# Four 64x64 gate products in place of two 128x128 ones in a linear recurrence, with one gate's heads swapped in PSUM

## The chip, the cores and the metric

The kernel runs on one core of a Trainium2 chip. The metric is the device time of one execution in microseconds (us); the median of the runs is compared. An execution taken by the profiler has a time of its own and, inside it, the span of the trace from its first instruction to its last.

## The reference

One layer of a decoder trunk: an RMS norm, one input projection, four groups of heads beside each other (two kinds of attention, a delta-rule recurrence "RWKV-7", and a gated linear recurrence "RG-LRU"), each multiplied with a gate of its own, and one output projection with a residual and a last norm. x is 1 x 1024 x 1024, in float32. The change is in the linear recurrence, whose 256 channels are four heads of 64:

```python
xc = causal_depthwise_conv(x, conv_w) + conv_b
xh = xc.reshape(b, s, N_HEADS, HEAD_DIM)
r = sigmoid(einsum('bsni,nij->bsnj', xh, w_a).reshape(b, s, c) + b_a)   # first gate
i = sigmoid(einsum('bsni,nij->bsnj', xh, w_x).reshape(b, s, c) + b_x)   # second gate
log_a = -8 * r * softplus(-lam)
a = exp(log_a)
u = sqrt(-expm1(2 * log_a)) * (i * xc)
h_t = a_t * h_(t-1) + u_t
```

Each head has a 64x64 matrix of its own for each of the two gates.

## The kernel before, in words

Everything of one core is one program, in which each engine has its instructions in an order that is written out by hand: the table ORDERS holds for TensorE (PE), VectorE (DVE), ScalarE (ACT), GpSimd (POOL) and SyncE (SP) the places of their instructions, and each one is held behind the one ahead of it. So an engine can't pass a waiting instruction; it waits there.

TensorE's order is mixed. The projections (pj_..., L402 and L989) are long rows of full 128x128 products that depend on little, and they stand between the short products of the RWKV recurrence, which depend on each other: for each chunk of 64 positions px (L758), then X (ScalarE copies px out of PSUM, L767), pu and py, then UV (VectorE copies pu, L783), ph, then UV of the next chunk (VectorE adds, L796), and so on. The linear recurrence runs in the same stretch of time, about 225 to 300 us from the start. Its function lru is called four times: for each pair of heads pr (128 channels, on 128 partitions) and each half hf of 512 positions.

Of one call, in the order of its data: the convolution makes xc (ACT L1048, then three DVE instructions, L1050); lwg holds the pair's two 64x64 matrices of a gate on the diagonal of a 128x128 matrix whose other quarters are zero, so that one float32 product (L1056) makes a gate's input for both heads; ScalarE takes each through a sigmoid out of PSUM (L1057) into rt, whose first half is r and whose second is i. Then tanh (L1065, into xb), exp (L1066), square (L1067), sqrt (L1069) on ScalarE, L1063, L1068 and L1070 on VectorE, the scan (L1073) and the product with the output gate (L1075), and y_out splits the result in two parts (L850, L851) and stores it. The PSUM banks of the gates, lg, come from a pool of two buffers (gbk) which other products use as well.

A float32 product takes two passes through the array, which the trace shows as two MATMUL records each; products of the rounded type (fp32r) take one.

Of the kernel before, what the change touches and what calls it, by code (L numbers as in the profile page):

```python
# [16 lines left out]
P = 128  # L17
# [25 lines left out]
for _name, _w in (  # L43
# [23 lines left out]
        "852-857 2018 2019 858-870 2026 871-895 2027-2057 896-914 2058-2089 915-919 2020 2021 920-932 2090-2093 "  # L67
        "933-941 2094-2101 942-947 2102-2109 948-953 2110-2121 954-956 2022 2023 2122-2125 957-967 2130-2133 "
        "2126-2129 968-983 2134-2141 984-992 2142-2149 993-996 2150-2153 997-1004 2154-2161 1005-1011 2162-2169 "
        "1012-1015 2170-2173 1016 1017 2024 2025 2174-2181 1018-1029 2182-2189 1030-1032 2190-2193 1033-1037 "  # L70
        "2194-2201 1038-1043 2202-2209 1044-1051 2210-2213 1052-1055 2214-2221 1056-1065 2222-2229 1066-1068 "
        "2230-2233 1069-1073 2234-2241 1074-1087 2242-2245 1088-1143 2246-2261 1144-1245 2262-2264 1246-1250 "
        "2265-2267 1251-1271 2275-2280 1272-1285 2288-2290 2268-2270 2291-2293 1286 2271-2274 2309-2311 2281-2283 "
        "1287 2312-2314 1288-1291 2284-2287 1292-1294 2330 2331 1295-1297 2294-2297 1298 1299 2332-2334 1300 1301 "
        "2302-2304 1302-1304 2335 2336 1305 1306 2298-2301 1307 1308 2337-2339 1309-1311 2305-2308 1312 1313 2363 "
        "2364 1314 1315 2315-2318 1316-1318 2365-2367 1319 1320 2323-2325 1321 1322 2368 2369 1323-1325 2319-2322 "
        "1326 1327 2370-2372 1328 1329 2326-2329 1330-1332 2340-2343 1333 1334 2396 2397 1335 1336 2348-2351 "
        "1337-1339 2398-2400 1340 1341 2356-2358 1342 1343 2401 2402 1344-1346 2344-2347 1347 1348 2403-2405 1349 "
        "1350 2352-2355 1351-1353 2359-2362 1354 1355 2373-2376 1356 1357 2437 2438 1358-1360 2381-2384 1361 1362 "
        "2439-2441 1363 1364 2389-2391 1365-1367 2442 2443 1368 1369 2377-2380 1370 1371 2444-2446 1372-1374 "  # L80
        "2385-2388 1375 1376 2392-2395 1377 1378 2406-2409 1379 1380 2414-2417 1381-1383 2478-2480 1384-1388 "
        "2422-2425 2410-2413 1389 2430-2432 1390 1391 2481-2483 1392 1393 2418-2421 1394-1396 2426-2429 1397 1398 "
        "2433-2436 1399 1400 2447-2450 1401 1402 2455-2458 1403 1404 2491-2493 1405-1407 2463-2466 1408 1409 "
        "2451-2454 1410 1411 2471-2473 1412 1413 2494-2496 1414 1415 2459-2462 1416 1417 2467-2470 1418-1420 "
        "2474-2477 1421 1422 2504-2506 1423-1425 2484-2486 1426-1429 2507-2509 1430-1432 2487-2490 1433-1436 "
        "2525-2527 1437-1440 2497-2499 1441-1443 2528-2530 1444-1447 2500-2503 1448-1450 2546 2547 1451-1453 "
        "2510-2513 1454 1455 2548-2550 1456 1457 2518-2520 1458-1460 2551 2552 1461 1462 2514-2517 1463 1464 "
        "2553-2555 1465-1467 2521-2524 1468 1469 2579 2580 1470 1471 2531-2534 1472-1474 2581-2583 1475 1476 "
        "2539-2541 1477 1478 2584 2585 1479-1481 2535-2538 1482-1485 2586-2588 1486-1490 2542-2545 1491-1494 "
        "2556-2559 1495-1499 2612 2613 1500-1504 2564-2567 1505-1508 2614-2616 1509-1513 2572-2574 1514-1518 2617 "  # L90
        "2618 1519-1522 2560-2563 1523-1527 2619-2621 1528-1532 2568-2571 1533-1536 2575-2578 1537-1541 2589-2592 "
        "1542-1546 2653 2654 1547-1550 2597-2600 1551-1555 2655-2657 1556-1559 2605-2607 1560-1564 2658 2659 "
        "1565-1569 2593-2596 1570-1573 2660-2662 1574-1578 2601-2604 1579-1583 2608-2611 1584-1587 2622-2625 "
        "1588-1592 2630-2633 1593-1596 2982 2983 1597-1620 2638-2641 2626-2629 1621 1622 2646-2648 2984 2985 "
        "2634-2637 2642-2645 1623-1626 2649-2652 1627-1630 2663-2666 1631-1634 2671-2674 1635-1639 2993 2994 "
        "1640-1644 2679-2682 1645-1647 2667-2670 1648-1652 2687-2689 1653-1656 2995 2996 1657-1660 2675-2678 "
        "1661-1664 2683-2686 1665-1669 2690-2693 1670-1673 3004 3005 2694-2696 2986-2988 2697-2700 3006 3007 "
        "2701-2703 2989-2992 2704-2706 3023 3024 2707-2709 2997-2999 2710-2713 3025 3026 2714-2716 3000-3003 "
        "2717-2719 3042 3043 2720 2721 3008-3011 2722-2724 3044 3045 2725 2726 3016-3018 2727 2728 3046 3047 2729 "
        "2730 3012-3015 2731 2732 3048 3049 2733 2734 3019-3022 2735-2737 3073 3074 2738 2739 3027-3030 2740 2741 "  # L100
        "3075 3076 2742 2743 3035-3037 2744 2745 3077 3078 2746-2748 3031-3034 2749 2750 3079 3080 2751 2752 "
        "3038-3041 2753 2754 3050-3053 2755 2756 3104 3105 2757 2758 3058-3061 2759-2761 3106 3107 2762 2763 "
        "3066-3068 2764 2765 3108 3109 2766 2767 3054-3057 2768 2769 3110 3111 2770 2771 3062-3065 2772-2774 "
        "3069-3072 2775 2776 3081-3084 2777 2778 3143 3144 2779 2780 3089-3092 2781 2782 3145 3146 2783 2784 "
        "3097-3099 2785-2787 3147 3148 2788 2789 3085-3088 2790 2791 3149 3150 2792 2793 3093-3096 2794 2795 "
        "3100-3103 2796 2797 3112-3115 2798-2800 3182 3183 2801 2802 3120-3123 2803 2804 3184 3185 2805-2807 "
        "3128-3131 2808 3116-3119 2809 2810 3186 3187 2811 2812 3136-3138 2813 2814 3124-3127 2815 2816 3188 3189 "
        "2817 2818 3132-3135 2819 2820 3139-3142 2821 2822 3151-3154 2823 2824 3221 3222 2825 2826 3159-3162 2827 "
        "2828 3223 3224 2829-2836 3167-3170 3155-3158 3225 3226 3175-3177 2837-2839 3163-3166 2840 2841 3227 3228 "
        "2842 2843 3171-3174 2844 2845 3178-3181 2846 2847 3190-3193 2848 2849 3284 3285 2850 2851 3198-3201 2852 "  # L110
        "3286 3287 2853 2854 3206-3209 2855 2856 3194-3197 2857 2858 3288 3289 2859 2860 3214-3216 2861 2862 "
        "3202-3205 2863 2864 3290 3291 2865 2866 3210-3213 2867 2868 3217-3220 2869 2870 3229-3232 2871 2872 3315 "
        "3316 2873 2874 3237-3240 2875 2876 3317 3318 2877 2878 3245-3248 2879 2880 3233-3236 2881 3319 3320 2882 "
        "2883 3253-3255 2884 2885 3241-3244 2886 2887 3321 3322 2888 2889 3249-3252 2890 2891 3256-3259 2892 2893 "
        "3292-3295 2894 2895 3370 3371 2896-2898 3300-3303 2899 2900 3308-3310 2901 2902 3296-3299 2903-2905 3372 "
        "3373 2906 2907 3304-3307 2908-2910 3311-3314 2911 2912 3323-3326 2913 2914 3389 3390 2915-2917 3331-3334 "
        "2918 2919 3339-3341 2920 2921 3327-3330 2922-2924 3391 3392 2925 2926 3335-3338 2927 2928 3342-3345 "
        "2929-2931 3374-3377 2932 2933 3432 3433 2934-2936 3382-3384 2937 2938 3434 3435 2939 2940 3378-3381 "
        "2941-2943 3385-3388 2944 2945 3393-3396 2946-2948 3443 3444 2949 2950 3401-3403 2951-2953 3445 3446 2954 "
        "2955 3397-3400 2956 2957 3404-3407 2958-2960 3436-3438 2961-2965 3439-3442 2966-2970 3447-3449 2971-2976 "  # L120
        "3450-3453 2977-2981 3260-3283 3346-3369 3408-3431 3454-3477"
# [38 lines left out]
        "1 0 2 4 7 8 3 9 5 10 6 11-21 23 24 27 31-35 22 36 25 28 26 37 29 38 30 49 39 40 63 41 43 64 42 44 80 48 "  # L160
        "81 45 46 82 50 51 47 52 53 83 84 59-61 54 62 55-57 85 75 86 65 58 66 87 67 69 68 70 88 74 71 72 89 90 "
        "178 91 73 92 179 93 76-79 94 190 180 181 95 182 184 183 185 189 96 97 186-188 98 99 191-193 195 194 272 "
        "196 273 197 198 200 100 101 199 102 235 103-107 110 111 202-204 108 274 275 205 114 206 207 115 208 109 "
        "209 210 219 211 220 112 221-224 201 212 225 118 119 213 226 236 227 229 113 239 228 231 232 230 122 233 "
        "234 214 116 237 240 215 241 242 117 216 217 123 245 238 120 218 124 248 243 125 246 121 247 276 249 254 "
        "244 250 277 126 251 257 127 252 278 255 128 256 258 259 279 263 129 260 266 253 281 280 264 261 130 265 "
# [1384 lines left out]
```

## Time and profile before

| What | Value |
|---|---|
| Median of 3 runs | 629.45 us (625.92 to 630.3) |
| Profiled execution | 629.03 us |
| Span of its trace | 627.1 us |
| Granted TensorE clock | 0.992 |
| PE busy | 608.5 us, 97% |
| DVE busy | 489.8 us, 78% |
| ACT busy | 390.7 us, 62% |
| POOL busy | 200.8 us, 32% |
| The gates' products (L1056) | 16 records of 591 to 664 ns, first at 238.3 us, last at 282.5 us |
| The gates' sigmoids (L1057) | 8 of 670 to 688 ns |

Times in a row are us from the span's start, durations us or ns as said there. A MATMUL record holds the whole way of a product through the array, so records overlap, and the distance from one start to the next says more than a duration. In brackets behind a row stands how long the engine sat idle before it, and what it waited for.

### The profile page before, as it was taken

To read this page: it belongs to the slowest core of one execution; us is meant where nothing else is said; L and a number is where in the kernel's file an instruction comes from. 1 tells how busy PE (TensorE), PEld (TensorE's weight loads), DVE (VectorE), ACT (ScalarE), POOL (GpSimd) and SP (SyncE) were. 2 spreads that over 40 slices of the span, in tenths; PEclk is the share of its full clock that TensorE was granted. 3 is DMA by queue.
4 is the path that set the end of the run, shared out by engine and by line. 5 is a ranking of instruction groups with operands and counts; after the bars stand their busy time and mean duration, and the time that the engine had idled before them with its cause. 6 is when DMAs were issued, how large, how long until landed. Compare 5 with 4: busy or idle time off the path is not lost.

```text
span 627.1 us, 11831 instructions
## 1 busy us (share of the span) xinstructions
PE 608.5 (97%) x4060; PEld 494.9 (79%) x4060; DVE 489.8 (78%) x1131; ACT 390.7 (62%) x722; POOL 200.8 (32%) x328
## 2 busy tenths in 40 slices
PE   8999999999999999999999999999999999999993
PEld 6867777778876687777888888879997788888882
DVE  6598687998996796978866988888774776857687
ACT  6797948451013378797534776567764657766575
POOL 2231421313113675444343220400223222322175
PEclk9999999999999999999999999999999899999997
DMA  8873766527351336721998665355498867763225
GB/s 288 305 220 87 193 176 152 143 101 183 108 165 62 103 99 222 241 100 71 254 300 270 202 211 159 134 169 168 143 273 298 261 207 248 256 197 135 84 102 201
DMA packets 86403, 114.35 MB, mean 182 GB/s; under 512 B 38151, under 2 KB 57927, under 8 KB 86344
## 3 DMA queue, kind: packets, MB, share of 16 engines
q1 hardware_dynamic: 69112, 57.81, 31.0%
q0 software_dynamic: 16656, 55.23, 26.1%
q8 instruction: 32, 0.52, 0.3%
q10 hardware_dynamic: 576, 0.56, 0.3%
q14 instruction: 27, 0.22, 0.1%
HBM read 79.31 MB, written 33.21 MB: 179 GB/s over the span
## 4 chain that ended last, share of the span: by engine, by line
PE 65%; DVE 13%; ACT 7%; DMA 7%; issue 6%; POOL 2%; SPq 1%; DVEq 0%; ACTq 0%; POOLq 0%
PE po L1351 9%; PE pj_fk L402 4%; PE pofx L1351 4%; PE pj_sg L402 4%; PE pj_fq L402 3%; PE pj_sq L402 3%; PE pj_rg L402 3%; PE pj_fg L402 3%; PE zsb L1174 3%; PE avfox L1256 3%; PE pj_v L402 3%; PE zfox L1174 2%; PE avsb L1256 2%; PE ptfox L1246 2%; DMA xr<-in_xT_dram 2%
## 5 line engine op out<-in xcount | busy, mean ns | idle before, releaser
L1351 PE MATMUL po<-woh,yc 128*128 128x512 f32 x192 | 69.6, 412 | 0.0
L1190 DVE TENSOR_TENSOR_SCAN atsb<-kp,atsb 128x128 f32<-128x128 f32 (+7 forms) x32 | 43.4, 1362 | 5.1 <-ACT atsb L1188 4.9
L1351 PE MATMUL po<-wol,yc 128*128 128x512 f32 x96 | 39.8, 414 | 0.0
L1222 ACT ACTIVATE atfox<-atfox,nb 128x128 f32<-128x128 f32 (+7 forms) x32 | 24.6, 770 | 23.9 <-DVE nb L1219 12.7
L1351 PEld LDWEIGHTS po<-woh,yc 128*128 128x128 f32 x192 | 34.8, 192 | 2.9
L1187 ACT ACTIVATE kp<-zsb 128x512 f32<-128x512 f32 (+3 forms) x48 | 23.6, 491 | 17.5 <-PE zsb L1174 17.0
L1252 DVE TENSOR_TENSOR PLfox<-ptfox,PHfox 128x512 fp32r<-128x512 f32 (+1 forms) x40 | 25.4, 636 | 10.4 <-ACT PHfox L1251 9.8
L1252 DVE TENSOR_TENSOR PLsb<-ptsb,PHsb 128x512 fp32r<-128x512 f32 (+1 forms) x40 | 25.1, 630 | 8.3 <-ACT PHsb L1251 7.5
L1251 ACT ACTIVATE PHsb<-ptsb 128x512 fp32r<-128x512 f32 (+1 forms) x40 | 22.1, 555 | 10.8 <-PE avsb L1256 5.9
L1251 ACT ACTIVATE PHfox<-ptfox 128x512 fp32r<-128x512 f32 (+1 forms) x40 | 21.9, 548 | 11.1 <-PE avfox L1256 9.7
L1174 PE MATMUL zsb<-KSsb,Q 128*128 128x512 f32 (+3 forms) x96 | 28.6, 357 | 0.0
L1174 PE MATMUL zfox<-KSfox,Q 128*128 128x512 f32 (+3 forms) x96 | 25.6, 349 | 2.2 <-DVE mx L1213 2.2
L1229 ACT ACTIVATE atfox<-atfox,sm 128x128 f32<-128x128 f32 (+7 forms) x32 | 23.4, 767 | 0.7 <-DVE sm L1226 0.7
L1188 ACT ACTIVATE atsb<-zsb 128x512 f32<-128x512 f32 (+3 forms) x48 | 23.4, 488 | 0.0
L749 POOL TENSOR_TENSOR Hp<-UV,PC 64x128 f32<-64x128 f32 x32 | 16.6, 518 | 21.3 <-DVE UV L796 17.6
L1174 PEld LDWEIGHTS zfox<-KSfox,Q 128*128 128x128 f32 x96 | 17.8, 191 | 6.2 <-DVE mx L1213 2.6
L1246 PE MATMUL ptsb<-ident,atsb 128*128 128x128 f32 x144 | 22.2, 272 | 0.4 <-DVE PLsb L1252 0.4
L1381 POOL TENSOR_TENSOR ac<-ac,fg 128x512 f32<-128x512 f32 x16 | 20.7, 1324 | 5.6 <-ACT ot L1359 5.6
L1213 DVE CUSTOM_DVE_ANT_0 atfox<-zfox,Fb 128x512 f32<-128x512 f32 (+3 forms) x40 | 20.9, 524 | 2.0 <-PE zfox L1174 1.8
L1246 PEld LDWEIGHTS ptfox<-ident,atfox 128*128 128x128 f32 x144 | 18.2, 140 | 5.5
L1246 PE MATMUL ptfox<-ident,atfox 128*128 128x128 f32 x144 | 22.2, 272 | 0.0
L1256 PE MATMUL avsb<-PLsb,VS 128*128 128x256 f32 x80 | 20.1, 286 | 0.9 <-DVE PLsb L1252 0.7
(547 smaller groups left out, 2161.6 us busy)
## 6 DMA issues: line engine op xcount, KB each, us to landing
yc<-yx_d POOLq DMA_DIRECT2D x16, 768.0 KB, 6.9
xn<-in_x_dram SPq DMA_DIRECT2D x8, 512.0 KB, 5.3
Q<-p_sq SPq DMA_DIRECT2D x64, 64.0 KB, 3.4
Q<-p_fq SPq DMA_DIRECT2D x64, 64.0 KB, 3.6
xt<-in_x_dram POOLq DMA_DIRECT2D x16, 256.0 KB, 6.1
out_dram<-ac SPq DMA_DIRECT2D x15, 256.0 KB, 2.1
xr<-in_xT_dram SPq DMA_DIRECT2D x6, 512.0 KB, 9.0
wor<-in_w_out_dram SPq DMA_DIRECT2D x9, 256.0 KB, 3.8
```

The costliest lines, as they stand in the source:

```text
L402: mm = nc.tensor.matmul(out[0:ww.shape[-1]], ww, xx[hf][:, k], start=(k == 0 and xx is xh and ww is wh), stop=(k == KT - 1 and ww is wl))
L1174: ((hi - c) / 2400, nc.tensor.matmul(z[:, c - lo:hi - lo], q, k, start=j == 0, stop=j == len(ops) - 1))
L1187: nc.scalar.activation(kp[:, lo:hi], z[:, 0:hi - lo], AF.Sigmoid, scale=-0.125)
L1188: nc.scalar.activation(at[:, lo:hi], z[:, 0:hi - lo], AF.Sigmoid, scale=0.125)
L1190: nc.vector.tensor_tensor_scan(rv, kp[:, 0:n][:, ::-1], rv, 0.0, op0=ALU.mult, op1=ALU.add)
L1222: exp = nc.scalar.activation(At[qb][:, 0:n], At[qb][:, 0:n], AF.Exp, bias=nb[:, qb:qb + 1], scale=0.125, accum_out=sm_[:, 0, qb:qb + 1])
L1229: nc.scalar.activation(At[qb][:, 0:n], At[qb][:, 0:n], AF.Copy, scale=sm_[:, 1, qb:qb + 1])
L1246: T.append((P / 1200, nc.tensor.transpose(pt[:, col:col + P], At[qb][:, (2 * m + j) * P:(2 * m + j + 1) * P], ident)))
L1251: nc.scalar.activation(PH[:, 0:w], pt[:, 0:w], AF.Copy)
L1252: nc.vector.tensor_tensor(PL[:, 0:w], pt[:, 0:w], PH[:, 0:w], op=ALU.subtract)
L1256: V.append(((c1 - c0) / 2400, nc.tensor.matmul(av[:, q0:256], VS[:, 2 * m + j, :], pp[:, c0:c1], start=m == 0 and j == 0 and pi == 0, stop ...
L1351: mm = nc.tensor.matmul(po, y, w, start=i == 0, stop=i == len(ops) - 1)
```

## The change

The four quarters of the array are used at the same time. The zero quarters of lwg are gone: it holds 64 columns a gate and pair, head o on the partitions 64 o to 64 o + 63, and GpSimd's memset of it is gone with them. Where two 128x128 products stood, four 64x64 ones stand, one for each head and gate. In the first gate head o goes from the row half o to the column half o of the array, in the second to the other half (to = o ^ j), so that the four products have four different quarters; the second gate's heads then lie in PSUM with their halves changed. ScalarE takes the first gate through its sigmoid in one instruction as before; the second gate takes two, each of 64 partitions, which read one half of the partitions and write the other, so that the heads are in their places again.

```diff
-            lwg = et(rp, "lwg", [P, 2, 2, P])
-            nc.gpsimd.memset(lwg, 0.0)
+            lwg = et(rp, "lwg", [P, 2, 2, 64])
             for pr in range(2):
                 for j in range(2):
                     for o in range(2):
-                        nc.sync.dma_start(lwg[64 * o:64 * o + 64, pr, j, 64 * o:64 * o + 64], a["lw"][j, 2 * pr + o])
+                        nc.sync.dma_start(lwg[64 * o:64 * o + 64, pr, j], a["lw"][j, 2 * pr + o])
...
-        ri = []
-        for j, b in enumerate(("b_a", "b_x")):
-            t = rt[:, j]
-            pg = gbk(f"lg{pr}{hf}{j}")
-            HELD[f"lg{pr}{hf}{j}"] = nc.tensor.matmul(pg, lwg[:, j], xc, start=True, stop=True)
-            nc.scalar.activation(t, pg, AF.Sigmoid, bias=pcol(b, pr))
-            ri.append(t)
-        r_, i_ = ri
+        pg = [gbk(f"lg{pr}{hf}{j}") for j in range(2)]
+        mm = None
+        for j in range(2):
+            for o in range(2):
+                to = o ^ j
+                m = nc.tensor.matmul(
+                    pg[j][64 * to:64 * to + 64], lwg[64 * o:64 * o + 64, j], xc[64 * o:64 * o + 64], start=True, stop=True)
+                if mm is None:
+                    HELD[f"lg{pr}{hf}0"] = m
+                else:
+                    follow(m, mm)
+                mm = m
+        r_, i_ = rt[:, 0], rt[:, 1]
+        nc.scalar.activation(r_, pg[0], AF.Sigmoid, bias=pcol("b_a", pr))
+        for o in range(2):
+            nc.scalar.activation(
+                i_[64 * o:64 * o + 64], pg[1][64 - 64 * o:128 - 64 * o], AF.Sigmoid,
+                bias=pcol("b_x", pr)[64 * o:64 * o + 64])
```

The places in ORDERS are counted anew. Apart from the rows of the change itself every engine keeps its order. The numbers behind a name are those of its buffer, and differ by the new count.

On TensorE at the first of the four places, before, the two products of the gates (lg) stand between products of a projection (pj_sk):

```order
L402 MATMUL pj_sk_1_1756<-xh_121,wl_sk_1_1720 128x512
L1056 MATMUL lg_3849<-xs_3843,lwg 128x512
L1056 MATMUL lg_3852<-xs_3843,lwg 128x512
L402 MATMUL pj_sk_0_1800<-xh_126,wh_sk_0_1789 128x512
L402 MATMUL pj_sk_0_1800<-xl_127,wh_sk_0_1789 128x512
```

And now:

```order
L402 MATMUL pj_sk_1_1756<-xh_121,wl_sk_1_1720 128x512
L1057 MATMUL lg_3848<-xs_3842,lwg 64x512 x2
L1057 MATMUL lg_3849<-xs_3842,lwg 64x512 x2
L402 MATMUL pj_sk_0_1800<-xh_126,wh_sk_0_1789 128x512
L402 MATMUL pj_sk_0_1800<-xl_127,wh_sk_0_1789 128x512
```

Four products on 64 partitions stand where two on 128 stood, and nothing around them has moved; the other three places read the same way.

On ScalarE at the first place, before, from the first gate's sigmoid (rt out of lg) past the tanh (xb), the split of an RWKV result (sg) and the exp to the second gate's sigmoid:

```order
L1057 ACTIVATE rt_3844<-lg_3849,pc 128x512
L1065 ACTIVATE xb_3838<-rt_3844,sp_137 128x512
L850 ACTIVATE sg_3633<-yo_3636 128x512
L1066 ACT_TABLE_LOAD
L1066 ACTIVATE rt_3844<-rt_3844,sp_137 128x512
...
L1048 ACTIVATE xs_3877<-xb_3873,pc 128x512
L1057 ACTIVATE rt_3844<-lg_3852,pc 128x512
L969 ACTIVATE sh_sk_1826<-sp_sk_1825 128x512
```

And now:

```order
L1065 ACTIVATE rt_3843<-lg_3848,pc 128x512
L1067 ACTIVATE rt_3843<-lg_3849,pc 64x512
L1075 ACTIVATE xb_3837<-rt_3843,sp_137 128x512
L850 ACTIVATE sg_3633<-yo_3636 128x512
L1076 ACT_TABLE_LOAD
L1076 ACTIVATE rt_3843<-rt_3843,sp_137 128x512
...
L1047 ACTIVATE xs_3879<-xb_3875,pc 128x512
L1067 ACTIVATE rt_3843<-lg_3849,pc 64x512
L968 ACTIVATE sh_sk_1826<-sp_sk_1825 128x512
```

The second gate's first half stands right behind the first gate, ahead of the tanh, and its second half stands where the whole second gate stood.

On ScalarE at the third and the fourth place it is the same, with the copy of a projection (sp_sv) or a load of ScalarE's function table behind the first half. At the fourth, before:

```order
L1057 ACTIVATE rt_3947<-lg_3952,pc 128x512
L1069 ACT_TABLE_LOAD
L1069 ACTIVATE xb_3907<-xb_3907 128x512
L995 ACTIVATE sp_sv_2029<-pj_sv_2004,rst_tk 128x256
L1057 ACT_TABLE_LOAD
L1057 ACTIVATE rt_3947<-lg_3955,pc 128x512
```

And now:

```order
L1065 ACTIVATE rt_3955<-lg_3960,pc 128x512
L1067 ACTIVATE rt_3955<-lg_3961,pc 64x512
L1079 ACT_TABLE_LOAD
L1079 ACTIVATE xb_3912<-xb_3912 128x512
L994 ACTIVATE sp_sv_2029<-pj_sv_2004,rst_tk 128x256
L1067 ACT_TABLE_LOAD
L1067 ACTIVATE rt_3955<-lg_3961,pc 64x512
```

One instruction is added ahead of the table load and the sqrt (xb), and the number of table loads stays the same.

170 rows, old and new, of the table ORDERS are left out of this document.

## The prediction

> **What bounds the kernel now.** I read the page's busy times first, then the tiles that the change touches, then the busy times of their stretch, then the chain of work that ended last there.
>
> ```profile
> PE 608.5 (97%) x4060; PEld 494.9 (79%) x4060; DVE 489.8 (78%) x1131; ACT 390.7 (62%) x722; POOL 200.8 (32%) x328
> L1056 PE MATMUL lg<-xs,lwg x16: 591/592/664, 238.5 to 282.5; 128*128 128x512 f32 x16
> L1057 ACT ACTIVATE rt<-lg,pc x8: 670/687/688, 239.6 to 286.6; 128x512 f32<-128x512 f32 x8
> 236.00:260.00 24.00, 23.88 (x238) 18.07 (x238) 19.66 (x31) 19.12 (x28) 11.31 (x19) 1.00 0.77 244
> 260.00:300.00 40.00, 38.63 (x484) 31.36 (x485) 32.75 (x64) 35.17 (x55) 17.06 (x28) 1.00 0.31 110
> ```
>
> TensorE is the bound by share, and the change is made on it. But the four places lie between 238 and 283 us, and the last two rows (length, then busy time of PE, weight loads, DVE, ACT and POOL) show that ScalarE is busy there as nowhere near its average of 62%: 19.12 of 24 us, then 35.17 of 40. In that second stretch PE sits idle for 1.37 us, by these rows and others like them:
>
> ```profile
> 263.16 0.45 PE L758 MATMUL ph<-UV,BKT 128*64 128x64 f32 x8 [0.24 <-DVE UV L783]
> 289.28 0.45 PE L758 MATMUL ph<-UV,BKT 128*64 128x64 f32 x8 [0.32 <-DVE UV L783]
> ```
>
> So PE here already waits for the recurrence's steps on other engines. The chain of waits shows who sets them (start, length, what):
>
> ```profile
> 272.29 0.69 ACT rt L1057
> ...
> 276.73 0.71 ACT xs L1048
> ...
> 281.31 0.95 PE lg L1056 x2
> 282.26 0.02 issue
> 282.28 0.03 ACT rt L1057
> 282.31 0.68 issue
> 282.99 1.28 ACT L1069
> ```
>
> Between these two rows of ScalarE the chain stays on it, table loads included (the third place), and at the fourth it runs through the first gate's product and sigmoid into the table load ahead of the sqrt (L1069). PE's 97% is the average; the sum has to be made on this chain.
>
> **What the change takes from PE.** At the first place the timeline of PE reads:
>
> ```profile
> 238.28 0.40 PE L402 MATMUL pj_sk<-xh,wl_sk 128*128 128x512 f32 x1
> 238.51 1.88 PE L1056 MATMUL lg<-xs,lwg 128*128 128x512 f32 x4
> 239.83 0.79 PE L402 MATMUL pj_sk<-xh,wh_sk 128*128 128x512 f32 x1
> 240.46 0.40 PE L402 MATMUL pj_sk<-xl,wh_sk 128*128 128x512 f32 x1
> ```
>
> A pj_sk product has the array for 0.23 us (238.28 to 238.51), so the one recorded at 239.83 had it from 240.46 - 0.23 = 240.23. The two gates held it from 238.51 to 240.23: 1.72 us, or 0.43 for each of four passes. Four places: 6.9 us, the most that could ever be won being less than that.
>
> The nearest thing to the new form with 512 columns in float32 is a pair of products on 32 rows each, pw and pa, in two row groups and two banks:
>
> ```profile
> 32.40 0.39 PE L402 MATMUL pj_k<-xh,wl_k1a 128*128 128x512 f32 x1
> 32.72 0.69 PE L498 MATMUL pw<-sm,wa 32*128 32x512 f32 x1
> 32.73 0.69 PE L501 MATMUL pa<-sm,wa 32*128 32x512 f32 x1
> 33.25 0.59 PE L498 MATMUL pw<-sm,wa 32*128 32x512 f32 x1
> 33.26 0.59 PE L501 MATMUL pa<-sm,wa 32*128 32x512 f32 x1
> 33.78 0.50 PE L402 MATMUL pj_k<-xh,wh_k1a 128*128 128x512 f32 x1
> 34.12 0.40 PE L402 MATMUL pj_k<-xl,wh_k1a 128*128 128x512 f32 x1
> ```
>
> Both first passes start 0.01 us apart, both second ones too: the passes of different tiles go side by side. By the same reckoning they held the array from 32.40 + 0.23 = 32.63 to 34.12 - 0.23 = 33.89, so 1.26 us: two passes of 0.43, and 0.40 for going into the divided array and out again, about half each (the first pass starts 0.09 late and lasts 0.10 longer). That four tiles in both directions work as well is shown by pu and py, 64x64 each, which lie in two banks and in the four quarters exactly as the new products do:
>
> ```profile
> 261.54 0.27 PE L758 MATMUL pu<-X,TR 64*64 64x64 f32 x2
> 261.56 0.27 PE L758 MATMUL py<-UV,TR 64*64 64x64 f32 x2
> 261.65 0.23 PE L758 MATMUL pu<-X,TR 64*64 64x64 f32 x2
> 261.66 0.23 PE L758 MATMUL py<-UV,TR 64*64 64x64 f32 x2
> ```
>
> Four passes start within some 0.02 us and the next four 0.11 later: 0.05 for 64 columns at the rate above (0.43 x 64 / 512), and 0.05 by which the first passes last longer. One after another, four passes alone would take 0.21. So a place takes 1.26 us instead of 1.72: **0.46 us less, 1.84 over four**. Bounds: 0.86 a place if going in and out were free (3.4 over four; the fourth is followed by pu and py, already divided, and comes near it), and 8 passes of 0.43 and 0.40, 3.84, if the four ran one after another (2.12 more, 8.5 over four).
>
> The Trainium skill, "TensorEngine Tiling (Array Packing)", section "Gotcha 1: PSUM Pressure", says that different row tiles can't use one PSUM bank at the same time, which speaks against this change: each gate's bank takes the products of both row halves. The rows of pu and py, whose two heads write one bank from both row halves, don't agree with it. I keep its result as a rival below.
>
> **What it adds to ScalarE.** A sigmoid of 64 partitions isn't cheaper for having half of them:
>
> ```profile
> L607 ACT ACTIVATE UV<-pv x8: 579/591/593, 58.9 to 231.0; 64x512 f32<-64x512 f32 x8
> L617 ACT ACTIVATE BKT<-bkt x8: 586/597/598, 60.3 to 236.3; 128x512 f32<-128x512 f32 x8
> L1260 ACT ACTIVATE ypsb<-avsb x16: 375/379/383, 348.2 to 471.8; 64x256 f32<-64x256 f32 x16
> ```
>
> So each place gets one more instruction of some 0.67 us. ScalarE starts the next one about 0.1 before the end of one that it doesn't need (xb and sg below: 0.72 long, 0.63 apart), so I take 0.57. Bounds: 0 where ScalarE sits idle, 0.69 where it doesn't. That one half of the partitions is read and the other written I cost at nothing: the attention's copies (L1260) do so, and their 0.38 for 256 columns is 0.21 under L607's 0.59 for 512, which is no more than half of it and a fixed part would be. A surcharge of theirs couldn't be over 0.08 (0.38 less half of 0.59).
>
> Place by place along the chain:
>
> ```profile
> 239.58 0.69 ACT L1057 ACTIVATE rt<-lg,pc 128x512 f32<-128x512 f32 x1 [1.16 <-PE lg L1056]
> 240.30 0.72 ACT L1065 ACTIVATE xb<-rt,sp 128x512 f32<-128x512 f32 x1
> 240.93 0.62 ACT L850 ACTIVATE sg<-yo 128x512 fp32r<-128x512 f32 x1
> 243.17 0.55 POOL L972 DMA_DIRECT2D p_sk<-sp_sk  x1 [1.01 <-DVE sp_sk L971]
> 247.92 0.69 DVE L968 TENSOR_TENSOR sp_sk<-pj_sk,rst_bc 128x512 f32<-128x512 f32 x1 [1.79 <-DMA p_sk<-sp_sk]
> 259.37 0.63 ACT L969 ACTIVATE sh_sk<-sp_sk 128x512 fp32r<-128x512 f32 x1 [1.72 <-DVE sp_sk L968]
> ```
>
> - First place. r needs both passes as before, and these start 0.2 late (going in): 0.2. The new half then stands ahead of tanh: r starts at 239.78, the half at 240.35, tanh at 240.92 instead of 240.30, so 0.62. Queued behind are sg (240.93), then on VectorE the product with sg (L851) and behind it a part of sp_sk, then POOL's store p_sk (243.17, waits for sp_sk), for whose landing VectorE waits at 247.92. From there VectorE works without a gap until PE waits for its UV (263.16). I let the **0.62** through whole.
> - Second place. The half falls into the 1.72 us that ScalarE waits before 259.37: **0**. If VectorE were early, ScalarE would pay 0.57 here too.
> - Third place. ScalarE has no gap there; X (L767), xs (L1048) and all behind move by **0.57**. PE's gain isn't on the chain, which goes past this product.
> - Fourth place. The gate's product is on the chain: 0.2 for going in, 0.57 for the half ahead of the table load and sqrt: **0.77**.
>
> Together 1.96 us later at PE's ph of 289.28, where PE waits for this chain. PE's 1.84 us become longer waits in front of the rows shown above. After that PE has projections that wait for nobody, so nothing gives the delay back, and the table loads keep their number.
>
> POOL's memset of lwg goes, 0: the loads of lwg on SP, which waited for it, stand behind a store that waits longer for VectorE, and what they bring is needed only at the first place. If that cover were gone, the loads would still be early by tens of us.
>
> **The sum** is made against the profiled execution, 629.03 us (its span 627.1, and 1.9 around it): 629.03 + 1.96 = **631.0**. It lies 0.4 under the median of the runs shown, less than they differ among themselves, so I make no shift.
>
> **Rivals.**
> - *PE's gain shows.* If the links of the chain have slack that the trace doesn't show (a landing of the store of 243.17 well ahead of 247.92 cuts the first term), PE is the bound and the whole 1.84 comes out: 627.2. For it: 23.88 of 24 us busy. Against it: the waits at 263.16 to 289.28. In between lies a draw.
> - *The four products run one after another*, so the change doesn't do what it says: 3.84 instead of 1.72 at each place, 8.5 us more on PE, of which its idle 1.4 can hide some: about 637, slower by over 1%. It decides as soon as a place takes over 1.72 + 0.49 = 2.2 us, when PE is later than the chain. Against it: the rows of pu and py; for it: none of these has 512 columns and 64 rows.
> - *The two row halves of a bank exclude each other.* Then the passes go 1, 2 with 3, 4 with the first one's second, 2 and 3 again, 4 again: five steps of 0.43 and 0.40, 2.55 a place, 0.83 more: 3.3 on PE. The first gate is ready two steps (0.86) later than forecast at the first and fourth place, where the chain goes through it: 631.0 + 1.7 = 632.7. That is what the skill's rule named above gives.
>
> **How the numbers follow.** Forecast 0.50; PE's gain shows, 0.35; banks exclude each other, 0.06; one after another, 0.04; the rest, 0.05, is that later waits for transfers fall otherwise, either way by some us. A measurement of this kernel tells about 1% (6.3 us) from no change. The most that PE can win is 3.4 us, so faster by over 1% needs the last case: 0.03. Slower by over 1% is the case of one after another and a little: 0.05. The rest, 0.92, is within 1%. For the range I take 627.2 less 1.2 for the bound of 3.4 and the runs' own spread, and 632.7 with the same on the other side: **626.0 to 634.0**; only the case of one after another is left out.
>
> **What would show it.** In the changed profile the four lg records of each pass should start within 0.03 us, a place should hold the array for 1.2 to 1.3 us, and the sigmoids should be 12 of 0.6 to 0.7 us, 4 more than before. The waits of ph, pu and px between 255 and 290 us should grow by 2 to 4 us in sum while PE's busy time falls. If these waits stay at 1.4 us in sum, PE's gain shows and the forecast is wrong by its sign; if lg passes start 0.4 us apart, one of the last two rivals holds.

## The result, and the profile after

| | Kernel before | Changed kernel |
|---|---|---|
| Median (19 runs each, same chips) | 626.74 us | 630.02 us |
| Ratio to before, 95% interval | | 1.0046, 1.003 to 1.0062 |
| Profiled execution, span | 629.03, 627.1 us | 630.08, 628.2 us |
| PE, DVE, ACT busy | 608.5, 489.8, 390.7 us | 605.7, 490.9, 394.8 us |

By the ratio the change costs 2.9 us (1.9 to 3.9), although TensorE has 2.8 us less to do. The ratio compares fast runs and leaves out one slow run of each kernel (634.52 and 637.67 us), so it is a little below the quotient of the medians. The cost is clear of the runs' noise and within the 1% that I had called no change. The lines below are of the changed kernel. A line of `lru` that was L1056 is L1057 there, and the sigmoid has become L1065 (first gate, r) and L1067 (second gate in two halves: I call `i_a` the first, which reads partitions 64 to 127 of the bank and writes 0 to 63, and `i_b` the second, the other way round). The rows show first the tile's groups (ns min/median/max, first and last start), then PE's timeline at the first place; the two rows ahead of the dots are from a view that ends at 237.4 us, the rows behind them from a longer one:

```profile
L1057 PE MATMUL lg<-xs,lwg x32: 589/614/640, 237.4 to 283.3; 64*64 64x512 f32 x32
L1067 ACT ACTIVATE rt<-lg,pc x8: 680/684/690, 239.2 to 289.1; 64x512 f32<-64x512 f32 x8
L1065 ACT ACTIVATE rt<-lg,pc x4: 687/688/690, 238.5 to 283.9; 128x512 f32<-128x512 f32 x4
```

```profile
237.05 0.39 PE L402 MATMUL pj_sk<-xh,wl_sk 128*128 128x512 f32 x1
237.37 0.66 PE L1057 MATMUL lg<-xs,lwg 64*64 64x512 f32 x4
...
237.37 1.09 PE L1057 MATMUL lg<-xs,lwg 64*64 64x512 f32 x8
238.39 0.50 PE L402 MATMUL pj_sk<-xh,wh_sk 128*128 128x512 f32 x1
238.72 0.39 PE L402 MATMUL pj_sk<-xl,wh_sk 128*128 128x512 f32 x1
```

Four products start between 237.37 and 237.40, the other four half a microsecond later: the four quarters do work side by side, with 512 columns too. By the same reckoning as in before, the place holds the array from 237.05 + 0.23 = 237.28 to 238.72 - 0.23 = 238.49, 1.21 us, where it was 1.72.

The same two stretches as before (length, then busy PE, weight loads, DVE, ACT, POOL; PE's granted clock), and PE's waits between 255 and 300 us:

```profile
236.00:260.00 24.00, 21.42 (x222) 15.63 (x221) 20.27 (x30) 18.86 (x26) 9.99 (x17) 1.00 0.73 228
260.00:300.00 40.00, 35.72 (x454) 29.15 (x457) 30.09 (x58) 35.30 (x53) 16.41 (x27) 0.96 0.29 105
```

```profile
256.03 1.09 PE L1057 MATMUL lg<-xs,lwg 64*64 64x512 f32 x8 [0.93 <-DVE xs L1049]
257.84 0.38 PE L988 MATMUL pj_sv<-wl_sv,xh 128*128 128x256 f32 x1 [0.72 <-DVE wl_sv L382]
...
276.85 0.45 PE L758 MATMUL px<-UV,GM 128*64 128x64 f32 x8 [0.59 <-DVE UV L796]
280.47 0.45 PE L758 MATMUL ph<-UV,BKT 128*64 128x64 f32 x8 [0.61 <-DVE UV L783]
...
288.78 0.45 PE L758 MATMUL px<-UV,GM 128*64 128x64 f32 x8 [1.74 <-DVE UV L796]
```

PE's busy time in the stretches falls from 23.88 to 21.42 and from 38.63 to 35.72 us, and its waits of over 0.15 us between 255 and 300 us grow from 1.25 to 6.16 us in sum (from 1.10 to 5.21 in the second profiles of the two kernels). Not all of that is won time: the products save 0.51 us a place, 2.0 in sum, and the rest goes with the lateness of the chain, behind which TensorE now waits. Two things in these rows were not in my forecast. The third place's piece on ScalarE is longer than 0.57 (start, length):

```profile
272.73 0.69 ACT L1065 ACTIVATE rt<-lg,pc 128x512 f32<-128x512 f32 x1
273.44 0.69 ACT L1067 ACTIVATE rt<-lg,pc 64x512 f32<-64x512 f32 x1
274.16 0.47 ACT L994 ACTIVATE sp_sv<-pj_sv,rst_tk 128x256 f32<-128x256 f32 x1
274.65 0.68 ACT L1067 ACTIVATE rt<-lg,pc 64x512 f32<-64x512 f32 x1
275.36 0.72 ACT L1075 ACTIVATE xb<-rt,sp 128x512 f32<-128x512 f32 x1
```

From r to tanh (xb) it is 275.36 - 272.73 = 2.63 us, 1.12 more than in before (273.80 - 272.29 = 1.51): no instruction starts before the one ahead of it has ended, where in before each overlapped by 0.10 to 0.12. And behind the wait of 1.74 us PE's clock drops to half (timeline, then windows of 3 us; the clock stands ahead of the last two numbers):

```profile
290.73 0.31 PE L988 MATMUL pj_sv<-wh_sv,xl 128*128 128x256 f32 x1
290.85 0.41 PE L988 MATMUL pj_sv<-wl_sv,xh 128*128 128x256 f32 x1
291.06 0.42 PE L988 MATMUL pj_sv<-wh_sv,xh 128*128 128x256 f32 x1
291.27 0.41 PE L988 MATMUL pj_sv<-wh_sv,xl 128*128 128x256 f32 x1
```

```profile
288.00:291.00 3.00, 2.12 (x32) 1.81 (x33) 2.84 (x5) 2.92 (x5) 2.21 (x3) 0.97 0.11 44
291.00:294.00 3.00, 3.00 (x26) 2.66 (x25) 2.53 (x7) 2.36 (x3) 0.99 (x2) 0.50 0.02 5
```

The pj_sv products go from 0.12 us apart to 0.21; reckoned by such windows of 1 us the half clock lasts 3.4 us. In before the clock is 1.00 there.

### The profile page after: what moved, and what is told of

It reads as the page before. It is cut to its first block, busy times and chain, and to the rows that moved or that the text cites. A ratio compares the mean times of both kernels' runs of the same rounds, so it can differ in the third digit from the quotient of the medians.

```text
span 628.2 us, 11864 instructions
## 1 busy us (share of the span) xinstructions
PE 605.7 (96%) x4076; PEld 492.5 (78%) x4076; DVE 490.9 (78%) x1131; ACT 394.8 (63%) x726; POOL 200.9 (32%) x327
## 4 chain that ended last, share of the span: by engine, by line
PE 75%; DVE 10%; ACT 7%; issue 4%; DMA 3%; POOL 0%; SPq 0%; DVEq 0%; ACTq 0%; POOLq 0%
PE po L1361 9%; PE pj_fk L402 4%; PE pj_r L402 4%; PE pj_rg L402 4%; PE pj_sg L402 4%; PE pj_lx L402 4%; PE pj_v L402 3%; PE pj_fq L402 3%; PE pj_sq L402 3%; PE pj_fg L402 3%; PE zsb L1184 3%; PE pj_k L402 3%; PE avfox L1266 3%; PE avsb L1266 2%; PE ptfox L1256 2%
```

## Where the lateness arises

Both kernels issue the same instructions in this stretch, so the start of one instruction in a trace less its start in before's first trace tells how late the kernel is there. The traces differ by -1.2 to +1.1 us already ahead of the first place, where only lwg's memset and loads are changed (two profiles of one kernel differ there by up to 0.6), so that is taken off. The steps between, in us: up to VectorE's product with sg (L851 of before, 241.57), to the product of i and xc (L1063, 253.97), to X of the third place (270.69), to the X behind its tanh (276.47), to sqrt (284.28), to the X at 291.54; last what has come together at the pj_sg product of 302.1. The kernels below the changed one are the experiments.

| Kernel | First place | Landings | Second | Third | Fourth | px wait and clock | At 302 us |
|---|---|---|---|---|---|---|---|
| before, second profile | 0.01 | -0.18 | 0.00 | -0.01 | 0.00 | 0.00 | -0.17 |
| changed | 0.72 | 1.17 | -0.20 | 1.10 | 0.80 | 1.23 | 4.83 |
| changed, second profile | 0.71 | 0.00 | -0.20 | 1.09 | 0.80 | 2.42 | 4.83 |
| products alone | 0.14 | 0.39 | -0.02 | -0.03 | 0.09 | 0.00 | 0.57 |
| ScalarE's part alone | 0.72 | 0.05 | -0.16 | 1.11 | 0.86 | 0.13 | 2.70 |
| halves in place | 0.57 | 0.64 | -0.20 | 0.94 | 0.66 | 1.02 | 3.63 |
| halves late | 0.15 | 0.94 | 0.23 | 0.95 | 0.08 | 0.33 | 2.68 |
| px filled | 0.72 | 0.27 | -0.20 | 1.09 | 0.80 | 1.48 | 4.26 |
| changed, xt early | 0.72 | 0.33 | -0.19 | 1.09 | 0.80 | 1.03 | 3.78 |
| refilled | 0.71 | 0.85 | -0.20 | 1.08 | 0.80 | 0.20 | 2.29 |
| refilled, xt early | 0.72 | 0.12 | -0.19 | 1.09 | 0.79 | 0.21 | 1.57 |
| before, xt early | 0.00 | 0.49 | -0.01 | 0.00 | 0.00 | 0.01 | 0.50 |
| before, refilled | 0.00 | -0.21 | 0.00 | 0.00 | 0.00 | 1.31 | -0.04 |

The columns for the places repeat to 0.02 us and are the change's; the column of landings (VectorE's wait for the store p_sk and ScalarE's for the load of lg) runs from -0.21 to 1.17, and in the second profiles of the same two kernels it is otherwise, so much of it is a scatter of transfers. Whether all of it is, the rows don't tell: the nine with the new products average 0.52 us, the five with the old ones 0.03.

## The experiments

**The two parts, each alone.** Products alone: the second gate through one sigmoid, in ScalarE's order of before.

```diff
-        for o in range(2):
-            nc.scalar.activation(
-                i_[64 * o:64 * o + 64], pg[1][64 - 64 * o:128 - 64 * o], AF.Sigmoid, ...)
+        nc.scalar.activation(i_, pg[1], AF.Sigmoid, bias=pcol("b_x", pr))
```

> The changed products (four of 64x64 side by side), but the second gate goes through one sigmoid of 128 partitions, as before, in ScalarE's order of before; the putting back is left out, so its heads stay exchanged. This is TensorE's part of the change alone. My forecast's step 'PE's gain is not on the chain': PE's busy time between 236 and 300 us falls by about 2 us, its waits there grow by as much less 0.4 for going into the divided array at two places, and the time is 1.000 to 1.001 of before. Rival 'PE's gain shows': 1.8 us less, 0.997. Rival 'the lateness comes from the products': about 1.004.

Measured: 0.9998 of before (0.9968 to 1.0028), and 0.57 us later at 302 us, not 1.8 earlier. Its windows and its wait ahead of px:

```profile
236.00:260.00 24.00, 22.48 (x240) 16.58 (x236) 20.91 (x31) 18.62 (x26) 10.51 (x18) 1.00 0.77 235
260.00:300.00 40.00, 37.14 (x486) 30.63 (x487) 32.73 (x64) 34.98 (x54) 17.28 (x29) 1.00 0.30 108
```

```profile
286.08 0.45 PE L758 MATMUL px<-UV,GM 128*64 128x64 f32 x8 [1.01 <-DVE UV L796]
```

PE is 2.9 us less busy, and none of it reaches the end. The interval of the times alone just holds the rival's 0.997; the trace speaks against it. Going into the divided array costs the chain 0.14 and 0.09 us at the first and fourth place.

ScalarE's part alone: the kernel before, with

```diff
-            nc.scalar.activation(t, pg, AF.Sigmoid, bias=pcol(b, pr))
+            if j == 0:
+                nc.scalar.activation(t, pg, AF.Sigmoid, bias=pcol(b, pr))
+            else:
+                for o in range(2):
+                    nc.scalar.activation(
+                        t[64 * o:64 * o + 64], pg[64 - 64 * o:128 - 64 * o], AF.Sigmoid, ...)
```

> The kernel before with its two 128x128 products, but the second gate's sigmoid in two halves that read one half of the partitions and write the other, in the changed kernel's order of ScalarE; this exchanges the heads of a gate that had them in place. This is ScalarE's part alone. Theory 'ScalarE's pieces on the chain': about 1.1 us at the first, third and fourth place, less what later waits give back: 1.004 to 1.005, as in the changed kernel. Rival 'the lateness comes from the products': 1.000. If PE's gain in the changed kernel had hidden a part of ScalarE's cost, this one is slower than the changed kernel, up to 1.0075.

Measured: 1.0016 (0.9987 to 1.0045). That is less than the 1.004 that I expected, but the interval holds both this and the rival's 1.000; the trace tells more. The three places cost what they cost in the changed kernel (0.72, 1.11, 0.86). What is missing is the last step: here px waits less, and PE's clock stays up.

```profile
290.03 0.45 PE L758 MATMUL px<-UV,GM 128*64 128x64 f32 x8 [0.99 <-DVE UV L796]
```

```profile
291.00:294.00 3.00, 2.62 (x44) 2.07 (x43) 2.81 (x7) 2.92 (x5) 0.61 (x1) 1.00 0.00 0
```

So the two parts don't add up: 0.57 and 2.70 us at 302 us alone, 4.83 together. Of the 1.6 us between, 1.1 stand in the column of px and the clock: ScalarE's lateness and TensorE's earliness fall into the same wait, and only together do they make it long enough in these profiles.

**Why the halves cost more than 0.57.**

```diff
-                i_[64 * o:64 * o + 64], pg[1][64 - 64 * o:128 - 64 * o], AF.Sigmoid,
+                i_[64 * o:64 * o + 64], pg[1][64 * o:64 * o + 64], AF.Sigmoid,
```

> The changed kernel, but each 64-partition sigmoid of the second gate writes the half of the partitions that it reads; the putting back of the heads is left out, so this gate's heads stay exchanged. The kernel before takes 626.7 us, the changed one 1.0046 of it, and its third place takes 2.63 us from the start of r's sigmoid to the start of tanh (1.51 before). Theory 'crossing': ScalarE loses its overlap with the instruction ahead and behind because the halves change partitions; then here the distances fall from 0.71 to 0.57, the third place to about 2.1 us, and the time to about 1.002. Theory 'half': any instruction on 64 partitions costs this; then 0.71, 2.6 us and 1.0046 stay. Theory 'not ScalarE': the distances may do what they like, the time stays at 1.0046.

Measured: 1.0041 (1.0014 to 1.0068), an interval that holds 1.002 and 1.0046 alike, so the rows have to decide. Its third place:

```profile
274.00 0.69 ACT L1065 ACTIVATE rt<-lg,pc 128x512 f32<-128x512 f32 x1
274.58 0.67 ACT L1067 ACTIVATE rt<-lg,pc 64x512 f32<-64x512 f32 x1
275.15 0.46 ACT L994 ACTIVATE sp_sv<-pj_sv,rst_tk 128x256 f32<-128x256 f32 x1
275.64 0.68 ACT L1067 ACTIVATE rt<-lg,pc 64x512 f32<-64x512 f32 x1
276.35 0.72 ACT L1075 ACTIVATE xb<-rt,sp 128x512 f32<-128x512 f32 x1
```

Neither theory holds as I put it. The half on partitions 0 to 63 has its overlap again on both sides (0.58 behind r, 0.57 to sp_sv); the one on 64 to 127 has none (0.49 behind the 0.46 of sp_sv, 0.71 to xb) although it no longer crosses. Crossing isn't the whole cause, and 64 partitions aren't a cause. What the rows of these kernels have in common: the overlap is lost on both sides of a half that writes from partition 64 on (i_b), and it is lost ahead of a half that reads PSUM from partition 64 on (i_a of the changed kernel, behind r, and behind xs and sh_sk in the kernel called halves late). Behind i_a it is lost to sp_sv and kept to xb, which reads SBUF (0.59 from start to start at the first place). Why this is so stays open. So the third place still costs 0.94, not 1.10 us: 2.35 us from r to tanh (276.35 - 274.00), where theory 'crossing' had 2.1.

**The half ahead of tanh and sqrt moved back.** In ScalarE's order i_a goes to i_b (its numbers 238, 248, 258, 268 to 239, 249, 259, 269).

```diff
-... 237 238 241 215 ... 123 246 239 120 ...     -... 267 268 264 130 269 ...
+... 237 241 215 ... 123 246 238 239 120 ...     +... 267 264 130 268 269 ...
```

> The changed kernel with the first half of the second gate's sigmoid moved in ScalarE's order from right behind the first gate's sigmoid to right ahead of the second half, where before had its one sigmoid. At the first place tanh and sg then start some 0.7 us earlier, at the fourth the table load ahead of sqrt as well, at the third nothing but 0.1 to 0.2 is won, since both halves stay ahead of tanh. Theory 'ScalarE's pieces on the chain': 1.3 us less than the changed kernel, 1.002 to 1.003. If one late step alone makes the lateness (the store behind the first place), more: 1.000 to 1.001; if ScalarE's total work there decides and not the place, 1.0046 stays.

Measured: 1.0056 (1.0025 to 1.0086), no better than the changed kernel and not the 1.002 to 1.003 that I expected. The first and fourth place do lose their cost (0.15 and 0.08), and at 302 us the kernel is 2.68 late, not 4.83. Later its PE waits 1.1 us for sp_sg at 331 us, 1.2 for a load at 356 and 1.6 at zfox. Waits like these also stand in other kernels (1.0 for sp_sg at 330 us in before refilled, 0.9 for the load at 352 in products alone, 1.3 there and 2.2 in before at zfox), so one profile doesn't tell what belongs to the order; why the time doesn't follow stays open.

**PE's wait ahead of px, filled with what stands next.** Eleven pj_sv products go ahead of px (2198):

```diff
-... 1030-1032 2198-2201 1033-1037 2202-2209 1038-1043 2210-2217 ...
+... 1030-1032 1033-1043 2198-2201 2202-2209 2210-2217 ...
```

> The changed kernel with eleven pj_sv products (0.12 us each, 1.3 in all) moved in TensorE's order from behind the px of the fourth place to ahead of it. In the changed kernel that px waits 1.74 us, and two us later TensorE runs at half its clock for some 3.3 us (0.50 between 291 and 294 us), and the chain loses 0.8 to 1.0 us more there than with ScalarE's part alone, where the same px waits 0.99 us and the clock stays at 1.00. Theory 'the wait costs clock': the longest wait of PE at this place falls to about 1.0 us or less, the granted clock stays at 1.00, and the chain is 0.8 to 1.0 us earlier at 294 us; the time is 1.003 of before. Rival 'the half clock hides under waits anyway': clock 1.00, but the place and the time (1.0046) stay as they are, because the moved products are missing as cover behind px.

Measured: 1.0061 (1.0034 to 1.0089). The wait ahead of px is short, but the gaps behind it now are empty:

```profile
289.13 0.45 PE L759 MATMUL px<-UV,GM 128*64 128x64 f32 x8 [0.42 <-DVE UV L797]
290.47 0.27 PE L759 MATMUL pu<-X,TR 64*64 64x64 f32 x2 [0.88 <-ACT X L768]
292.13 0.28 PE L759 MATMUL ph<-UV,BKT 128*64 128x64 f32 x2 [1.20 <-DVE UV L784]
```

The clock fell all the same:

```profile
291.00:294.00 3.00, 1.87 (x20) 1.75 (x21) 2.53 (x7) 2.69 (x4) 0.73 (x2) 0.74 0.02 5
294.00:297.00 3.00, 3.00 (x35) 2.46 (x35) 1.05 (x2) 1.72 (x4) 0.64 (x2) 0.69 0.56 219
```

So one long wait isn't needed: here 2.5 us of waiting in three pieces within 3.4 us stood ahead of the half clock. The experiment moved the idle time and took none away.

**The load that both kernels wait for at 484 us.** In the first pair of profiles the changed kernel gets 2.3 of its 4.8 us back between 480 and 494 us, at VectorE's wait for xt (VectorE's timeline; the first row is of before, the second of the changed kernel, then their second profiles in the same order):

```profile
483.83 0.69 DVE L1353 TENSOR_TENSOR ac<-po,xt 128x512 f32<-128x512 f32 x1 [3.16 <-DMA xt<-in_x_dram]
```

```profile
486.02 0.69 DVE L1363 TENSOR_TENSOR ac<-po,xt 128x512 f32<-128x512 f32 x1 [1.61 <-DMA xt<-in_x_dram]
```

```profile
482.58 0.69 DVE L1353 TENSOR_TENSOR ac<-po,xt 128x512 f32<-128x512 f32 x1 [2.58 <-DMA xt<-in_x_dram]
```

```profile
488.20 0.69 DVE L1363 TENSOR_TENSOR ac<-po,xt 128x512 f32<-128x512 f32 x1 [2.90 <-DMA xt<-in_x_dram]
```

The edit in GpSimd's order, of before and (one number lower each) of the changed kernel:

```diff
-... 179 299 262 261 259 180 260 ...
+... 179 299 259 262 261 180 260 ...
```

> The kernel before, with GpSimd's load of xt00 (256 KB) issued ahead of the two loads of yc10 (768 KB each) and not behind them. In before VectorE's first product with xt waits 3.16 us for it (at 483.8 us), PE then 2.2 us (zfox), and PE's clock is 0.50 from 487 to 490 us. In the changed kernel, 3.6 us later at this point, these are 1.61 and 0.7 us and the clock stays at 1.00: this is where it gets back 2.3 of its 3.6 us. Theory 'given back': the load lands early, the waits and the half clock go, and before becomes 2 to 4 us faster, 0.994 to 0.997. Rival: the load is limited by the traffic and not by its place in the queue, or yc10 is late instead: 1.000.

> The changed kernel with the same earlier load of xt00. Theory 'given back': with the wait gone from both kernels nothing takes the change's lateness back, so this one gains less than the kernel before does from the same edit, and stands 3.5 to 5 us (0.6 to 0.8%) above it: 1.001 to 1.004 of before. Rival 'nothing is given back': both gain the same, and it stands 2.9 us (0.46%) above that one.

> The kernel before, unchanged, for a second profile: it shows which waits recur. If the wait for xt (3.16 us), PE's zfox wait (2.2) and the half clock behind it belong to the kernel, they are here within 1 us; if they are chance, they aren't. The stretch from the first place to 300 us should repeat to 0.5 us, with no wait of PE over 0.5 us in it.

> The changed kernel, unchanged, for a second profile. If the wait of some 1.7 us ahead of px at the fourth place and the half clock behind it belong to the change, both are here again (four of four profiles with the changed products and the first half ahead of sqrt, against none of four without). The stretch from the first place to 300 us should again be 3.5 to 5 us longer than in before.

Measured: before with the early load 0.9979 (0.9953 to 1.0004), the changed kernel with it 1.0027 (1.0002 to 1.0053). The wait is gone in both (480.54 us, no wait, in before). They gain about the same, 0.0021 and 0.0019, some 1.3 us where I had expected 2 to 4 in before. That goes with the rival 'nothing is given back', but the intervals leave room for a difference of over 2 us between the two gains. The second profiles say the same: before waits 2.58 us again, but without the half clock (PE's zfox wait is 1.6 there, 2.2 in the first), and the changed kernel waits 2.90 us too, runs at half clock a second time behind it (492.9 to 496.3 us) and gets nothing back: its span is 4.7 us longer than before's first, 6.8 longer than before's second. So the 2.3 us of the first pair don't recur in the second. The wait ahead of px and the half clock were there again:

```profile
288.22 0.70 PE L758 MATMUL px<-UV,GM 128*64 128x64 f32 x8 [1.74 <-DVE UV L796]
```

```profile
288.00:291.00 3.00, 2.78 (x30) 2.35 (x30) 2.43 (x4) 2.92 (x5) 1.71 (x3) 0.52 0.13 49
291.00:294.00 3.00, 3.00 (x24) 2.66 (x25) 2.04 (x6) 1.79 (x3) 0.39 (x1) 0.50 0.12 46
```

**PE's waits filled with later products, the row behind moved up.** From px of 288.78 on, the gaps ahead of px, pu, ph, px, pu, ph, px, pu and the last py hold 14, 8, 8, 8, 5, 10, 4, 6 and 5 products (3, 5, 6, 8, 4, 10, 3, 5 and 14 before the edit).

```diff
-... 1030-1032 2198-2201 1033-1037 2202-2209 1038-1043 2210-2217 1044-1051 2218-2221 ...
+... 1030-1043 2198-2201 1044-1051 2202-2209 1052-1059 2210-2217 1060-1067 2218-2221 ...
```

> The changed kernel with the pj_sv products from the fourth place on moved forward in TensorE's order, so that the gaps in front of px, pu, ph and px hold 14, 8, 8 and 8 of them (3, 5, 6 and 8 in the changed kernel); by the last py of this recurrence 10 more are done. Other than in px_filled, later products follow up into the places that get empty. Theory 'TensorE's gain lies in its waits and can be fetched': its waits of 1.74 us and less fill with products that else come after 300 us, the clock stays at 1.00, and the time is 2 to 2.5 us less than the changed kernel's: 1.0005 to 1.0015 of before. Rival 'the chain alone decides': the waits of PE get shorter but the pj_sv products only wait for their PSUM bank instead, or ScalarE and VectorE are late by the same: 1.0046 stays.

> The same new order of pj_sv in the kernel before, as a control. PE's idle time at this place is 0.15 and 0.32 us there, so nothing is to be filled: px and ph of the chain stand behind more products and get up to 1.2 us later, while as much falls away after 300 us. Theory 'TensorE's gain lies in its waits': 1.000 within 0.002, and the refilled changed kernel gains clearly more by this edit than before does. Rival 'the order is simply better': both gain the same 2 us.

> The changed kernel with both edits, pj_sv forward and the early load of xt00. The early load alone brought the kernel before to 0.9979 and the changed one to 1.0027. If both add up, this one is at 0.998 to 0.9995, level with the kernel before with the early load alone; if TensorE's whole gain of 2 us came out on top, it would be at 0.996.

Measured: the changed kernel refilled 1.0015 (0.999 to 1.004), at the upper end of the range that I gave; before refilled 1.0026 (0.9994 to 1.0058), which isn't told from before, while the 2 us less of the rival are outside; the changed kernel with both edits 0.9963 (0.9939 to 0.9987), less than the 0.998 to 0.9995 of adding both up and at the value that I gave for TensorE's whole gain. Of the refilled changed kernel:

```profile
290.04 0.45 PE L760 MATMUL px<-UV,GM 128*64 128x64 f32 x8 [0.42 <-DVE UV L798]
```

```profile
291.00:294.00 3.00, 3.00 (x48) 2.60 (x47) 2.81 (x7) 2.92 (x5) 0.63 (x1) 1.00 0.02 5
```

The clock stays at 1.00, 48 product records lie in the window where 26 did, and at 302 us the kernel is 2.29 late, not 4.83: 1.0 from the clock (0.20 in the column, not 1.23), and 1.15 from pj_sv products that are done already (3.44 late at the X of 291.54, 2.29 behind the last pj_sv); the rest is the landings. In before the same edit finds nothing to fill: px only comes 1.31 us later, and at 302 us it stands where it stood. So time was lying in the waits and could be fetched, but only with work that else comes later. The kernel with both edits is faster than before (0.4%, 0.1 to 0.6); against before with the early load alone (0.9979, 0.9953 to 1.0004) the intervals overlap, so that the new products are worth anything by themselves isn't shown.

**How often the clock falls.** The mean granted clock of a run is on record for most runs, not only for the profiled ones. All 14 profiles show half clock at the kernel's end. In seven of them it comes nowhere else, and their mean is 0.994 or more; in the other seven it also comes earlier, and their mean is 0.993 or less. By this mark the clock fell in 13 of 18 runs of the changed kernel, 9 of 12 of halves in place, 10 of 12 of px filled and 8 of 12 of the changed one with xt early, but only in 4 of 12 of products alone, 2 of 12 of ScalarE's part alone, 3 and 2 of 12 of the two refilled changed kernels, 3 and 1 of 12 of before refilled and before with xt early, and 28 of 93 of before itself (these are 2.9 us longer than its others). So the change makes the fall frequent, and neither part alone does; at which place it falls, the mean doesn't tell. Halves late has it in 9 of 12 too, although its one profile doesn't, so that profile is not typical of its runs. And ScalarE's part alone costs time without it: its ten runs at 0.994 or more average 628.9 us, the 23 such runs of before made beside them 626.8.

## Why the prediction was right, and where not

It said 631.0 us, 626 to 634, no change that 1% can tell, slower by 2.0 us. The median is 630.02, and the change costs 2.9 us (1.9 to 3.9). That the time came out within 1.0 us is in part luck: I counted from 629.03, 2.3 above before's median over more runs, and took the cost too small. The direction and the reason, ScalarE's pieces on the chain, hold; two terms don't.

- **Four products side by side, 1.26 us a place:** right, 1.21, all four within 0.03 us. Both rivals that gave more (one after another; row halves of a bank exclude each other) are out. The second followed from the Trainium skill, "TensorEngine Tiling (Array Packing)", section "Gotcha 1: PSUM Pressure"; each of the two banks here is written from both row halves at once, into different halves of its partitions, so the trace doesn't agree with that rule.
- **PE's gain is not on the chain:** right, by the trace of the products alone (0.57 us later at 302 us); their time, 0.9998, agrees, with an interval that just reaches the rival.
- **"PE's 1.84 us become longer waits":** this step failed in what it leaves out. A longer wait was taken to cost nothing. The waits grew by 4.9 us (4.1 in the second profiles), not by 2 to 4, and behind those of the fourth place TensorE runs at half its clock for 3.4 us (6.8 in the second profile), which makes the chain 1.0 to 2.4 us later. It is in all five profiles with the new products and i_a ahead of sqrt, the refilled ones apart, and at this place in none of the others.
- **ScalarE, first place 0.62:** 0.72. **Fourth place 0.77:** 0.80 (0.09 for going in, not 0.2, and 0.71 for the half, not 0.57). **Second place 0:** -0.2.
- **Third place 0.57:** 1.09. The term was mis-sized: I took one more piece with an overlap of 0.1; it is one piece without, 0.71, and three neighbours that lose theirs, some 0.13 each. The mistake was to count on the overlap. "That one half of the partitions is read and the other written I cost at nothing" is 0.15 of it, by the 0.94 of halves in place; most of the rest goes with the half that writes from partition 64 on, which is there without crossing too. Before's trace had a row with the loss, which I read for its length alone:

```profile
404.72 0.63 ACT L381 ACTIVATE wh_fv<-wr_fv 128x512 fp32r<-128x512 f32 x1 [1.20 <-PE pj_fg L402]
405.38 0.38 ACT L1260 ACTIVATE ypsb<-avsb 64x256 f32<-64x256 f32 x1
405.78 0.63 ACT L1164 ACTIVATE VS<-vw 128x512 fp32r<-128x512 f32 x1
406.32 0.47 ACT L1187 ACTIVATE kp<-zsb 128x384 f32<-128x384 f32 x1
```

  The crossing copy starts 0.03 behind the end of the one ahead and 0.02 passes behind it, while VS overlaps kp by 0.09.
- **"Nothing gives the delay back":** not contradicted. Both kernels gain about the same from the early load, which leaves over 2 us open either way; the first pair of profiles gave 2.3 us back, the second nothing.

With the measured terms the sum is 0.72 - 0.20 + 1.09 + 0.80 = 2.4, and 1.0 to 2.4 for the clock, 3.4 to 4.8 us where the clock falls; the times say 1.9 to 3.9, over runs of which 13 in 18 have a fall and before's own have one now and then. How much of the rest is the scatter of the landings isn't shown.

## What to carry to other kernels

A faster engine off the chain gets waits for its gain; to have the gain, move work that comes later and depends on nothing into these waits, as much as the rest behind it can follow up, and check the granted clock behind TensorE's longer waits. Before putting data back by way of partitions, look in the trace at the distance from one start to the next around such instructions, not at their length. Two profiles of one kernel show what a landing is worth; one doesn't.

## What the runs showed of the hardware

- **TensorE's clock can fall to half after 1.5 to 2.2 us of idle time within a window of 3.4 us, and it changes on a grid.** 1.74 us ahead of px with 0.35 behind it were followed by 3.4 us at 0.50, the second time by 6.8; 0.42, 0.88 and 1.20 within 3.4 us did it too; the kernel before has it itself, behind the 2.2 us at zfox of its first profile. 1.02 and 0.66 (halves late) or 0.99 and 0.29 (ScalarE's part alone) didn't do it. The length of one wait doesn't decide: 1.28 us at zfox in products alone did it, 1.63 there in before's second profile didn't. In each trace the changes of the clock lie whole multiples of 3.413 us apart: in the changed kernel it is 0.50 from 290.84 to 294.25 and 1.00 for 327.68 us behind that, 96 times 3.413. Counted by the windows of this grid, the idle time of PE in the window ahead of a fall (those at the kernel's end left out) was 1.45 to 2.21 us; but windows with 1.35 to 1.85 us idle had none behind them, so within this range something else decides, which stays open. Two neighbouring windows of products alone, then two of before's second profile (idle 1.61 and 1.66 us in the first of each; the clock stands ahead of the last two numbers):

```profile
485.47:488.88 3.41, 1.80 (x8) 1.02 (x7) 2.52 (x9) 3.36 (x9) 0.54 (x1) 1.00 0.84 267
488.88:492.29 3.41, 3.41 (x13) 3.02 (x14) 3.21 (x12) 0.17 (x1) 2.12 (x4) 0.50 0.86 246
483.75:487.17 3.42, 1.76 (x7) 0.88 (x6) 2.05 (x6) 3.37 (x9) 0.45 (x2) 1.00 0.79 250
487.17:490.58 3.41, 3.10 (x18) 2.74 (x19) 3.34 (x16) 1.01 (x3) 2.23 (x4) 1.00 0.71 195
```

  The lengths of 3.4 and 6.8 us and the grid go with the free-running window of about 3.4 us of which the Trainium skill tells, "TensorE: Matmul & The Clock Gate", section "Part 1: The HAM clock gate (the "warmup" mystery)". Its rule of thumb in "HAM oscillation — how this bites in real kernels", no idle gaps over about 3.4 us, isn't enough here: half as much did it.
- **ScalarE's overlap of 0.10 to 0.12 us** between neighbours is lost on both sides of an instruction that writes from partition 64 on, and ahead of a sigmoid that reads PSUM from partition 64 on: in the rows compared the next starts 0.01 to 0.03 us behind the end. The Trainium skill, "ScalarE: Activation LUTs", section "What ACT_TABLE_LOAD costs", gives an overlap of about 0.093 us for neighbours, which the other rows bear out, and no such exception.
